# The first scale and shift of a two-layer decoder computed in quarters instead of halves

## The chip, the cores and the metric

One Trainium2 chip, one core. The metric is the device time of one execution in microseconds (us). The engines are TensorE (PE in the rows, its weight loads PEld), VectorE (DVE), ScalarE (ACT), GpSimd (POOL) and SyncE (SP), which here issues most loads.

## The reference

Two decoder layers over 256 prompt tokens and 8 sequences of 4 sample tokens (288 token columns), model width 1024, everything in float32. Layer 0 mixes tokens with retention, layer 1 with a gated delta rule; each is followed by a gated convolutional FFN. Ahead of every sub-layer stands a normalisation whose scale and shift come from a conditioning vector `c`, one per sequence:

```
mod = silu(c) @ w_ada[l] + b_ada[l]
sh1, sc1, g1, sh2, sc2, g2 = split(mod, 6)
h = x * rsqrt(mean(x*x) + EPS) * norm_mix[l]
h = h * (1 + sc1) + sh1
proj = h @ w_ret_in           # q, k, v, gate of the retention
```

The change concerns the first `sh1`, `sc1`, the `h` made of them, and the first columns of `proj`.

## The kernel before

Tokens lie along the free axis: `x` is 8 tiles of 128 channels by 288 tokens. A weight block is 128x1024 float32, 512 KB. For precision each weight block and each activation is split in a high part and a rest (`whi`, `wlo`, `hh`, `hl`), and a product is three rounds of matmuls, `whi`*`hh`, `whi`*`hl`, `wlo`*`hh`, over the 8 channel tiles: 24 matmuls of 128x288. ScalarE makes `whi` (a cast), VectorE `wlo` (a subtraction).

The scale and shift (`ada`) need 14 chunks of 8 blocks. A block gives matmuls into `adaP`, four column groups side by side; when a chunk is complete, ScalarE copies it out (`adaev`), TensorE transposes it (`adaT`), and VectorE adds the bias into `mod`. The retention's first `h` needs two chunks. Chunk 0 holds scale and shift of channel tiles 0 to 3, chunk 1 those of tiles 4 to 7. `modulated` then makes `am` (scale times norm weight), `hs` (the sample tokens, three steps), and for each tile `h` (scaled), `hh` (shifted, cast; ScalarE) and `hl` (the rest; VectorE, GpSimd for the sample tokens). `rb_ret` is the reciprocal root of each token's mean square (`st_ret` its sums).

`first_h` is the start: chunk 0, `h` of tiles 0 to 3, then `EARLY = 3` products begun on these four tiles while chunk 1 is worked off, `h` of tiles 4 to 7, the second half of the begun products. `retention` takes the begun products first: `rt` and `qk` are the rotation of q and k, `qm` masked copies of q, `pA` the scores of head 0, `pv` and `pg` the products of values and gates, `S` blocks of the recurrent state, `pO` its first reader.

The order of the loads is a plan (`plan_weights`); `load` issues them on SyncE in that order as buffers come free: `more` has `RAW_START = 8` places for the start's blocks and then 3, `raw` has 4. `advance` splits weight blocks up to 2 ahead (`LOOK`). Within an engine the order of instructions is settled when the kernel is built: a scheduling layer places what the program records, so an instruction can stand ahead of one recorded earlier. Each engine then runs its list in order.

## Time and profile before

| | us |
|---|---|
| median of 3 runs | 1236.23 (1225.26 to 1239.33) |
| the profiled execution | 1233.65 |
| its span, first to last instruction | 1231.9 |
| TensorE busy | 1164.1, 95% |
| VectorE, ScalarE, GpSimd busy | 870.3, 608.8, 327.7 |
| DMA | 269.08 MB, 218 GB/s over the span |

The profiled execution's own time is 1.75 us more than its span. Times in the rows count from the span's start.

### The profile page before, as it was taken

The page shows a single profiled execution, that of the slowest core. Times are in us where ns is not written, and L with a number is a line of the kernel's source. Part 1 is how long each engine was busy: PE and PEld are TensorE (multiplying, and loading weights), DVE is VectorE, ACT ScalarE, POOL GpSimd, SP SyncE. Part 2 cuts the span into 40 slices and gives each one's busy share as a digit, 9 for nine tenths or more (in the row PEclk, how much of TensorE's full clock was granted, in tenths as well). Part 3 has the DMA queues.
Part 4 walks back from the last instruction along what each step waited for, and adds up shares of the span by engine and source line. Part 5 has one row for each costly group of instructions (what it writes and reads, how often), then busy time and mean ns, then how long its engine had stood idle before and what let it go on. Part 6 is the DMA issues. An engine that isn't in the chain of part 4 may idle for free.

```text
span 1231.9 us, 24934 instructions
## 1 busy us (share of the span) xinstructions
PE 1164.1 (95%) x9486; PEld 1049.1 (85%) x9486; DVE 870.3 (71%) x2003; ACT 608.8 (49%) x1256; POOL 327.7 (27%) x507
## 2 busy tenths in 40 slices
PE   6999999999999999999989998988899899999996
PEld 2879798797969999997777788977889699999996
DVE  3657574765766666667679888797965588777775
ACT  2444534344445544444674645744544365555553
POOL 0213142251302122222252223233222113223232
PEclk9999999999999999999999988988989899999998
DMA  9998696877699556557636641533434897777621
GB/s 365 345 332 324 227 336 233 313 246 242 211 314 393 189 171 190 171 181 259 209 92 211 223 144 63 159 129 115 131 103 129 298 357 239 258 254 253 196 76 56
DMA packets 97480, 269.08 MB, mean 218 GB/s; under 512 B 26816, under 2 KB 29088, under 8 KB 97232
## 3 DMA queue, kind: packets, MB, share of 16 engines
q1 hardware_dynamic: 87456, 234.57, 57.2%
...
q8 instruction: 75, 1.23, 0.4%
q14 instruction: 45, 0.37, 0.1%
...
## 4 chain that ended last, share of the span: by engine, by line
PE 78%; DVE 12%; DMA 3%; ACT 3%; issue 2%; POOL 1%; SPq 0%; POOLq 0%; ACTq 0%; DVEq 0%
PE down L535 17%; PE fg L535 12%; PE fv L535 12%; PE pg L535 4%; PE pv L535 4%; PE adaP L455 4%; PE p L535 3%; PE gv L535 2%; PE gz L535 2%; DVE wlo L417 2%; DVE mp L1332 2%; PE gk L535 2%; PE pO L898 1%; PE pU L917 1%; PE pS L868 1%
## 5 line engine op out<-in xcount | busy, mean ns | idle before, releaser
L417 DVE TENSOR_TENSOR wlo<-more,whi 128x1024 fp32r<-128x1024 f32 x138 | 171.1, 1241 | 74.5 <-ACT whi L416 63.2
L416 ACT CAST whi<-more 128x1024 fp32r<-128x1024 f32 x138 | 144.3, 1047 | 136.5 <-PE down L535 53.1
L417 DVE TENSOR_TENSOR wlo<-raw,whi 128x1024 fp32r<-128x1024 f32 x123 | 155.4, 1267 | 70.6 <-ACT whi L416 48.4
L416 ACT CAST whi<-raw 128x1024 fp32r<-128x1024 f32 x123 | 128.1, 1044 | 133.5 <-PE down L535 32.8
L716 POOL TENSOR_TENSOR x<-x,dt 128x32 f32<-128x32 f32 x159 | 100.6, 634 | 135.2 <-DVE dt L714 134.1
L712 DVE SCALAR_TENSOR_TENSOR x<-down,mod,x 128x256 f32<-128x256 f32 x160 | 76.6, 479 | 51.3 <-PE down L535 50.5
L591 POOL TENSOR_TENSOR fal<-cv,fah 128x288 fp32r<-128x288 f32 x44 | 41.6, 945 | 215.7 <-ACT fah L590 180.7
L535 PE MATMUL down<-fal,whi 128*128 128x288 f32 x352 | 64.0, 294 | 0.0
L535 PE MATMUL down<-fah,whi 128*128 128x288 f32 x352 | 62.3, 294 | 0.0
L535 PE MATMUL down<-fah,wlo 128*128 128x288 f32 x352 | 62.1, 294 | 0.0
L535 PE MATMUL fg<-hh_ffn,whi 128*128 128x288 f32 x352 | 58.9, 300 | 1.2 <-ACT hh_ffn L637 1.2
L918 DVE SCALAR_TENSOR_TENSOR S<-S,pU 128x512 f32<-128x512 f32 x64 | 42.2, 684 | 24.2 <-PE pU L917 24.1
L535 PE MATMUL fv<-hh_ffn,whi 128*128 128x288 f32 x352 | 58.7, 298 | 0.0
L535 PEld LDWEIGHTS fg<-hh_ffn,whi 128*128 128x128 f32 x352 | 50.6, 189 | 5.6 <-ACT hh_ffn L646 2.6
L535 PE MATMUL fg<-hh_ffn,wlo 128*128 128x288 f32 x352 | 55.0, 296 | 0.0
L535 PE MATMUL fv<-hh_ffn,wlo 128*128 128x288 f32 x352 | 54.8, 295 | 0.0
L535 PE MATMUL fv<-hl_ffn,whi 128*128 128x288 f32 x352 | 54.3, 295 | 0.0
L535 PE MATMUL fg<-hl_ffn,whi 128*128 128x288 f32 x352 | 54.0, 295 | 0.0
L535 PEld LDWEIGHTS fv<-hh_ffn,whi 128*128 128x128 f32 x352 | 50.5, 189 | 2.5 <-ACT ftail L947 1.2
L535 PEld LDWEIGHTS down<-fah,whi 128*128 128x128 f32 x352 | 51.8, 188 | 0.8 <-ACT whi L416 0.4
L535 PEld LDWEIGHTS down<-fal,whi 128*128 128x128 f32 x352 | 52.3, 188 | 0.2 <-issue 0.2
L535 PEld LDWEIGHTS down<-fah,wlo 128*128 128x128 f32 x352 | 52.0, 188 | 0.0
...
## 6 DMA issues: line engine op xcount, KB each, us to landing
...
S<-in_sr SPq DMA_DIRECT2D x16, 1024.0 KB, 8.0
out_rs<-S POOLq DMA_DIRECT2D x16, 1024.0 KB, 8.1
...
```

Of the source, the lines that this page charges most:

```text
L416: nc.scalar.copy(hi[:, :c], r)
L417: nc.vector.tensor_tensor(lo[:, :c], r, hi[:, :c].bitcast(F32), ALU.subtract)
L455: nc.tensor.matmul(self.adaP[32 * g : 32 * g + 32, 0:256], lhsT=self.cs[:, k, :], rhs=rv[:, :, g, :], start=(k == 0), stop=(k == KT - 1), ...
L535: self.nc.tensor.matmul(out, lhsT=av[:, k, c0 : c0 + m], rhs=b[:, k, :], start=(k0 == 0 and i == 0), stop=(k1 == kts and i == len(seq) - 1))
L591: (nc.gpsimd if pool_lo else nc.vector).tensor_tensor(lo, src, hi.bitcast(F32), ALU.subtract)
L712: nc.vector.scalar_tensor_tensor(xm[:, :TP], p[:, :TP], g[:, 0:1], xm[:, :TP], ALU.mult, ALU.add)
L716: (nc.vector if gate == 11 and last and m == KT - 1 else nc.gpsimd).tensor_tensor(xv, xv, t, ALU.add)
L868: nc.tensor.matmul(pS, lhsT=kt[:, j, c * P : (c + 1) * P], rhs=vt[:, j, :], start=(j == 0), stop=(j == 1))
L898: nc.tensor.matmul(pO4[32 * g : 32 * g + 32, :], lhsT=qm[:, c, 4 * bb + g, :], rhs=S[bb, c][:, g, :], start=(bb == 0 and c == 0), stop=Fal ...
L917: nc.tensor.matmul(pU, lhsT=kms[g][:, c * P : (c + 1) * P], rhs=vst, start=True, stop=True)
L918: nc.vector.scalar_tensor_tensor(S[bb, c][:, g, :], S[bb, c][:, g, :], gamma4, pU, ALU.mult, ALU.add)
L1332: nc.vector.tensor_tensor(m, Ti[:, 0:k, :].rearrange("p j c -> p c j").unsqueeze(1).to_broadcast([P, w, 8, k]), X[:, 0:k, i:k].rearrange(" ...
```

## The change

The weights of the first scale and shift are laid out anew (`wadq`): four quarters of four blocks, each quarter holding scale and shift of two channel tiles; a block holds two rows of 128 input channels by 512 columns. A quarter's matmuls have 128 columns instead of 256 and are twice as many (`ada_quarter`); per quarter there is one copy, one transpose and two bias additions. `first_h` goes over the quarters: scale and shift, `h` of two tiles, these tiles' part of the products begun so far, then new products from their beginning. `FIRST_W` says how many weights are begun behind each quarter (1, 1, 3, 0), five in all instead of three; they get banks of their own (`START_TAGS`). The start has 15 places for blocks instead of 8. The loads' order is 4 blocks, 1 weight, 4 blocks, 1 weight, 4 blocks, 3 weights, 4 blocks. The split of the first weight of the next phase is kept behind the start's last `hh` and `hl` on its engines (`issue_after`).

```diff
-CST_AT = 4
+CST_AT = 6
-EARLY = 3
-LATE = 1
+FIRST_W = (1, 1, 3, 0)
+EARLY = sum(FIRST_W)
+START_TAGS = ["c", "mm", "s", "mm", "e"]
-RAW_START = 8
+RAW_START = 15
...
-        second, step = ada(1), -(-KT // (EARLY - LATE))
-        plan = [ada(0)]
-        for i in range(EARLY):
-            plan[0] += wl("wri", i, 1) + second[i * step : (i + 1) * step]
+        plan = [[]]
+        for q, n in enumerate(FIRST_W):
+            plan[0] += [("ada", q - 4, k, A["wadq"][4 * q + k]) for k in range(4)]
+            plan[0] += wl("wri", sum(FIRST_W[:q]), n)
...
-            nc.scalar.copy(hi[:, :c], r)
-            nc.vector.tensor_tensor(lo[:, :c], r, hi[:, :c].bitcast(F32), ALU.subtract)
+            with ExitStack() as behind:
+                if self.plan[n][4] and self.plan[n - 1][4] == 0:
+                    for i in self.first_end:
+                        behind.enter_context(self.tc.issue_after(i))
+                nc.scalar.copy(hi[:, :c], r)
+                nc.vector.tensor_tensor(lo[:, :c], r, hi[:, :c].bitcast(F32), ALU.subtract)
...
+    def ada_quarter(self, q, k, r):
+
+        nc = self.nc
+        rv = r.rearrange("p (a g f) -> p a g f", a=2, g=4)
+        for a in range(2):
+            for g in range(4):
+                nc.tensor.matmul(
+                    self.adaP[32 * g : 32 * g + 32, 0:P], lhsT=self.cs[:, 2 * k + a, :], rhs=rv[:, a, g, :],
+                    start=(k == 0 and a == 0), stop=(k == 3 and a == 1), skip_group_check=True,
+                )
+        if k == 3:
+            ev = self.tmp.tile([P, T], F32, tag="t288", name="adaev", bufs=T288)[:, 0:P]
+            nc.scalar.copy(ev, self.adaP[:, 0:P])
+            pt = self.aux("adaT")
+            nc.tensor.transpose(pt[:, 0:P], ev, self.ident)
+            pt = pt[:, 0:P].rearrange("p (m r) -> p m r", r=32)[:, :, 0:9]
+            for m, m0 in ((0, 8 + 2 * q), (2, 2 * q)):
+                bias = self.prm("bada")[:, m0 : m0 + 2].unsqueeze(2).to_broadcast([P, 2, 9])
+                nc.vector.tensor_tensor(self.mod[:, m0 : m0 + 2, :], pt[:, m : m + 2], bias, ALU.add)
...
-        for i in range(EARLY):
-            if i == EARLY - LATE:
-                self.ada_due()
-                self.modulated(0, 0, 1, "ret", *h, rb, KT // 2, KT)
-            w = self.weights("wri")
-            begun.append((self.mmt(f"pe{i}")[:, 0:T], w))
-            self.product(*begun[-1], KT, 0, P, h, 0, KT // 2)
...
+        for q, n in enumerate(FIRST_W):
             self.ada_due()
+            if q == 0:
+                rb = self.now(self.token_rsqrt(self.ssum, 1.0 / DM, "ret"))
+            if q == 2:
+                self.load_cst(rc, "cst_a", nc.scalar, self.mod[:, 2, 0:1])
+            self.modulated(0, 0, 1, "ret", *h, rb, 2 * q, 2 * q + 2)
...
+            for i, (p, w) in enumerate(begun):
+                if q == 3 and i == FREE:
+                    self.hold = False
+                    self.advance()
+                self.product(p, w, KT, 0, P, h, 2 * q, 2 * q + 2)
+            for i in range(n):
+                w = self.weights("wri")
+                begun.append((self.aux(f"pe{len(begun)}", START_TAGS[len(begun)])[:, 0:T], w))
+                self.product(*begun[-1], KT, 0, P, h, 0, 2 * q + 2)
```

What the built order makes of it, at two places. VectorE before, from the second chunk's `mod` on (`wlo<-more` is the third weight's split, the last two those of the fourth and fifth weight):

```order
L468 TENSOR_TENSOR mod<-adaT,prm 128x36 x2
L618 SCALAR_TENSOR_TENSOR am_ret<-mod,prm 128x36
L628 TENSOR_TENSOR hs_ret<-x,am_ret 128x128
L632 TENSOR_TENSOR hs_ret<-hs_ret,rb_ret 128x128
L642 SCALAR_TENSOR_TENSOR h_ret<-x,am_ret,rb_ret 128x256
L417 TENSOR_TENSOR wlo<-more_201,whi 128x1024
L636 TENSOR_TENSOR hs_ret<-hs_ret,mod 128x128
L642 SCALAR_TENSOR_TENSOR h_ret<-x,am_ret,rb_ret 128x256 x3
L648 SCALAR_TENSOR_TENSOR hl_ret<-h_ret,mod,hh_ret 128x256 x4
L417 TENSOR_TENSOR wlo<-more_203,whi 128x1024
L417 TENSOR_TENSOR wlo<-more_205,whi 128x1024
```

VectorE of the changed kernel, quarter 2 from its first `h` to the `mod` of quarter 3 (the three `wlo` are those of the third to fifth weight):

```order
L673 SCALAR_TENSOR_TENSOR h_ret<-x,am_ret,rb_ret 128x256
L667 TENSOR_TENSOR hs_ret<-hs_ret,mod 128x64
L424 TENSOR_TENSOR wlo<-more_144,whi 128x1024
L679 SCALAR_TENSOR_TENSOR hl_ret<-h_ret,mod,hh_ret 128x256
L673 SCALAR_TENSOR_TENSOR h_ret<-x,am_ret,rb_ret 128x256
L424 TENSOR_TENSOR wlo<-raw,whi 128x1024 x2
L679 SCALAR_TENSOR_TENSOR hl_ret<-h_ret,mod,hh_ret 128x256
L499 TENSOR_TENSOR mod<-adaT,prm 128x18 x2
```

Three weight splits instead of one now stand between the two tiles' steps. TensorE before, from the end of chunk 1 (`pe_259`, `pe_295`, `pe_357` are the begun products 1 to 3):

```order
L455 MATMUL adaP<-raw,c 32x256 x4
L455 MATMUL adaP<-more_169,c 32x256 x4
L455 MATMUL adaP<-more_195,c 32x256 x4
L464 MATMUL adaT<-cst,adaev 128x128 x2
L535 MATMUL pe_357<-hh_ret,whi 128x288 x4
L535 MATMUL pe_357<-hl_ret,whi 128x288 x4
L535 MATMUL pe_357<-hh_ret,wlo 128x288 x4
L535 MATMUL pe_259<-hh_ret,whi 128x288
```

TensorE of the changed kernel, around quarter 3 (`pe_251` to `pe_452` are the begun products 1 to 5; the first row waits for the last `hl` of quarter 2):

```order
L566 MATMUL pe_251<-hl_ret,whi 128x288
L566 MATMUL pe_251<-hh_ret,wlo 128x288 x2
...
L566 MATMUL pe_452<-hl_ret,whi 128x288 x6
L566 MATMUL pe_452<-hh_ret,wlo 128x288 x6
L487 MATMUL adaP<-raw,c 32x128 x16
L487 MATMUL adaP<-more_171,c 32x128 x8
L487 MATMUL adaP<-more_173,c 32x128 x8
L495 MATMUL adaT<-cst,adaev 128x128
L566 MATMUL pe_251<-hh_ret,whi 128x288 x2
L566 MATMUL pe_251<-hl_ret,whi 128x288 x2
```

Before, the second chunk's matmuls stand ahead of the third begun product; now those of quarter 3 stand behind all five begun products' work on quarters 0 to 2.

## Rows read from the trace of the kernel before

**Rows 1.** The page: busy us, share of the span and instructions of each engine; and the shares of the chain that ended last, by engine.

```profile
PE 1164.1 (95%) x9486; PEld 1049.1 (85%) x9486; DVE 870.3 (71%) x2003; ACT 608.8 (49%) x1256; POOL 327.7 (27%) x507
...
PE 78%; DVE 12%; DMA 3%; ACT 3%; issue 2%; POOL 1%; SPq 0%; POOLq 0%; ACTq 0%; DVEq 0%
```

**Rows 2.** Windows by stage: stretch and length in us, busy us of each engine with its instructions, granted TensorE clock, busy share of the DMA engines, GB/s.

```profile
7.90:24.30 16.40, 12.27 (x87) 5.11 (x87) 7.29 (x25) 3.58 (x9) 0.21 (x1) 1.00 1.02 393
24.30:39.50 15.20, 13.17 (x95) 7.43 (x95) 7.11 (x18) 4.44 (x9) 1.40 (x5) 0.89 1.02 406
39.50:51.00 11.50, 11.50 (x84) 11.29 (x85) 10.61 (x19) 6.01 (x8) 4.22 (x5) 1.00 0.83 309
51.00:344.00 293.00, 292.43 (x2178) 251.27 (x2176) 186.23 (x326) 129.77 (x226) 83.86 (x104) 1.00 0.77 275
```

**Rows 3.** Timeline of the start: start in us, duration in us, engine, line, operation, output and inputs, shapes, count; in brackets the engine's idle time before it and what ended it.

```profile
7.93 1.08 PE L455 MATMUL adaP<-more,c 128*32 128x256 f32 x8 [7.93 <-ACT sq L606]
9.33 0.20 PEld L455 LDWEIGHTS adaP<-more,c 128*32 128x32 f32 x8 [1.20 <-DMA more<-in_wada]
...
13.20 0.18 PEld L455 LDWEIGHTS adaP<-more,c 128*32 128x32 f32 x2 [1.08 <-DMA more<-in_wada]
...
14.20 1.44 PE L566 MATMUL st_ret<-ones,ssum 128*128 128x1 f32 x6
...
15.68 0.16 DVE L547 TENSOR_SCALAR rsv_ret<-st_ret 128x3 f32<-128x3 f32 x1 [4.54 <-PE st_ret L566]
...
17.47 1.49 PE L575 MATMUL rb_ret<-cst,tr_ret 128*128 128x128 f32 x6
...
18.89 1.25 PE L455 MATMUL adaP<-more,c 128*32 128x256 f32 x16
...
20.48 1.05 ACT L416 CAST whi<-raw 128x1024 fp32r<-128x1024 f32 x1
```

**Rows 4.** Timeline from the last matmuls of chunk 1 to the second half of the begun products; columns as in rows 3.

```profile
33.70 1.24 PE L455 MATMUL adaP<-more,c 128*32 128x256 f32 x15
35.00 0.37 ACT L461 COPY adaev<-adaP 128x256 f32<-128x256 f32 x1 [7.46 <-PE adaP L455]
...
35.42 0.44 PE L464 MATMUL adaT<-cst,adaev 128*128 128x128 f32 x2 [0.48 <-ACT adaev L461]
35.90 0.30 DVE L468 TENSOR_TENSOR mod<-adaT,prm 128x36 f32<-128x36 f32 x2 [7.11 <-PE adaT L464]
...
36.89 0.47 DVE L642 SCALAR_TENSOR_TENSOR h_ret<-x,am_ret,rb_ret 128x256 f32<-128x256 f32 x1
...
37.28 1.22 DVE L417 TENSOR_TENSOR wlo<-more,whi 128x1024 fp32r<-128x1024 f32 x1
38.42 0.28 DVE L636 TENSOR_TENSOR hs_ret<-hs_ret,mod 128x128 f32<-128x128 f32 x1
...
38.94 1.71 ACT L646 ACTIVATE hh_ret<-h_ret,mod 128x256 fp32r<-128x256 f32 x4
...
39.50 1.61 PE L535 MATMUL pe<-hh_ret,whi 128*128 128x288 f32 x10
40.00 1.68 DVE L648 SCALAR_TENSOR_TENSOR hl_ret<-h_ret,mod,hh_ret 128x256 fp32r<-128x256 f32 x4
...
42.12 2.36 DVE L417 TENSOR_TENSOR wlo<-more,whi 128x1024 fp32r<-128x1024 f32 x2 [0.44 <-ACT whi L416]
```

**Rows 5.** Timeline of TensorE: starts of the fourth, fifth and sixth product, and of the scores of head 0.

```profile
44.62 1.21 PE L535 MATMUL p<-hh_ret,whi 128*128 128x288 f32 x8
...
47.81 1.23 PE L535 MATMUL pv<-hh_ret,whi 128*128 128x288 f32 x8
...
51.01 1.23 PE L535 MATMUL pv<-hh_ret,whi 128*128 128x288 f32 x8
...
52.61 1.47 PE L787 MATMUL pA<-qk 128*128 128x256 f32 x8
```

**Rows 6.** Timeline of the rotation of q: two of VectorE's five steps, and GpSimd's part.

```profile
44.83 0.46 DVE L744 TENSOR_TENSOR rt<-pe,cst_a 128x288 f32<-128x288 f32 x1 [0.34 <-PE pe L535]
45.20 0.45 DVE L745 TENSOR_TENSOR rt<-pe,cst_a 128x288 f32<-128x288 f32 x1
...
46.51 0.90 POOL L749 TENSOR_TENSOR qk<-rt,rt 128x288 f32<-128x288 f32 x1 [6.94 <-DVE rt L747]
...
47.49 2.29 POOL L794 TENSOR_TENSOR qm<-qk,cst_b 128x256 f32<-128x256 f32 x2
```

**Rows 7.** TensorE's longest wait behind the first landing (total us, times, longest us, up to 45 us), and two windows behind it, columns as in rows 2.

```profile
PE pe L535 <- ACT hh_ret L637: 2.7, 1, 2.7
...
26.00:29.50 3.50, 3.50 (x19) 1.16 (x18) 1.90 (x3) 1.09 (x2) 0.00 (x0) 0.52 1.03 407
29.50:32.00 2.50, 2.50 (x18) 2.21 (x18) 0.00 (x0) 0.00 (x0) 0.00 (x0) 0.99 1.03 418
```

**Rows 8.** Loads of the recurrent state and of the rotation's table: DMA issues up to 60 us (count, KB each, median us to landing); SyncE's first issue of `S` in its timeline; the reader of `S` in the chain that ended last (start, us).

```profile
S<-in_sr SPq DMA_DIRECT2D x2, 1024.0 KB, 7.9
...
cst_a<-in_cst_a ACTq DMA_DIRECT2D x1, 288.0 KB, 4.7
...
45.53 0.38 SPq L882 DMA_DIRECT2D S<-in_sr  x1
...
71.35 1.72 PE pO L898 x16
```

More of the change, by code (lines that the diff above doesn't have):

```diff
@@ L202, in lay_out @@
     wa = np.concatenate([inp["w_ada"][0], inp["w_ada"][1], inp["w_ada_final"]], 1)
-    wa[:, : 2 * DM] = wa[:, : 2 * DM].reshape(DM, 2, 2, 512)[:, ::-1].transpose(0, 2, 1, 3).reshape(DM, 2 * DM)
-    d["wada"] = wa.reshape(KT, P, 14, 1024).transpose(2, 0, 1, 3).reshape(14 * KT, P, 1024)
+    d["wada"] = wa[:, 2 * DM :].reshape(KT, P, 12, 1024).transpose(2, 0, 1, 3).reshape(12 * KT, P, 1024)
+    w = wa[:, : 2 * DM].reshape(4, 2, P, 2, 4, 256)[:, :, :, ::-1]
+    d["wadq"] = w.transpose(4, 0, 2, 1, 3, 5).reshape(16, P, 1024)
     parts = {
@@ L310, in plan_weights @@
         A = self.A
-        ada = lambda ch: [("ada", ch, k, A["wada"][ch * KT + k]) for k in range(KT)]
+        ada = lambda ch: [("ada", ch, k, A["wada"][(ch - 2) * KT + k]) for k in range(KT)]
         wl = lambda name, i0, n: [("w", name, 0, A[name][i]) for i in range(i0, i0 + n)]
@@ L452, in ada_step @@
             self.adaP = self.aux("adaP", self.ada_tag)
+        if ch < 0:
+            return self.ada_quarter(ch + 4, k, r)
         rv = r.rearrange("p (c g f) -> p c g f", c=2, g=4)
         for g in range(4):
-            nc.tensor.matmul(
+            i = nc.tensor.matmul(
                 self.adaP[32 * g : 32 * g + 32, 0:256], lhsT=self.cs[:, k, :], rhs=rv[:, :, g, :],
@@ L458, in ada_step @@
             )
+            if ch == 2 and k == 0 and g == 0:
+                self.tc.keep_in_program_order(i)
         if k == KT - 1:
@@ L465, in ada_step @@
             pt = pt[:, 0:256].rearrange("p (m r) -> p m r", r=32)[:, :, 0:9]
-            for m, m0, n in ((0, 8 + 4 * ch, 4), (4, 4 * ch, 4)) if ch < 2 else ((0, 8 * ch, 8),):
-                bias = self.prm("bada")[:, m0 : m0 + n].unsqueeze(2).to_broadcast([P, n, 9])
-                nc.vector.tensor_tensor(self.mod[:, m0 : m0 + n, :], pt[:, m : m + n], bias, ALU.add)
+            m0, n = 8 * ch, 8
+            bias = self.prm("bada")[:, m0 : m0 + n].unsqueeze(2).to_broadcast([P, n, 9])
+            nc.vector.tensor_tensor(self.mod[:, m0 : m0 + n, :], pt, bias, ALU.add)
+    def ada_quarter(self, q, k, r):
[16 more added lines that the diff above has]
+                nc.vector.tensor_tensor(self.mod[:, m0 : m0 + 2, :], pt[:, m : m + 2], bias, ALU.add)
     def spawn(self, gen):
@@ L645, in modulated @@
             else:
-                nc.scalar.activation(hi[:, m, :TP], h, AF.Identity, bias=shift[:, i, 0:1])
+                ends = [nc.scalar.activation(hi[:, m, :TP], h, AF.Identity, bias=shift[:, i, 0:1])]
             if lo is not None:
-                nc.vector.scalar_tensor_tensor(lo[:, m, :TP], h, shift[:, i, 0:1], hi[:, m, :TP].bitcast(F32), ALU.add, ALU.subtract)
-        self.ada_due(FILLS[2])
+                ends.append(nc.vector.scalar_tensor_tensor(lo[:, m, :TP], h, shift[:, i, 0:1], hi[:, m, :TP].bitcast(F32), ALU.add, ALU.subtract))
+        if rb_given is None:
+            self.ada_due(FILLS[2])
+        self.first_end = [i.ins for i in ends]
     def h_tiles(self, name):
@@ L662, in first_h @@
         h = self.h_tiles("ret")
[L663 to L667 removed]
         begun = []
         self.hold = True
[L670 to L686 removed]
+        rb = None
+        for q, n in enumerate(FIRST_W):
+            self.ada_due()
+            if q == 0:
[3 more added lines that the diff above has]
+            self.modulated(0, 0, 1, "ret", *h, rb, 2 * q, 2 * q + 2)
+            if q == 3:
+                self.load_cst(rc, "cst_r", nc.scalar, self.mod[:, CST_AT, 0:1])
+                self.load_cst(self.cp, "cst_b", nc.scalar, self.mod[:, CST_AT, 0:1])
+                self.load_cst(self.cp, "prm_b", nc.scalar, self.mod[:, CST_AT, 0:1])
+            for i, (p, w) in enumerate(begun):
[7 more added lines that the diff above has]
+                self.product(*begun[-1], KT, 0, P, h, 0, 2 * q + 2)
         self.hold = False
```

16 lines of the change are left out of this document (1 added, 15 removed).

## The prediction

> **What bounds the kernel now.** I read the page first. TensorE is busy for 95% of the span and carries 78% of the chain that ended last [rows 1], so a stage gains time only where TensorE stands idle or runs slowly. The windows by stage tell where that is [rows 2]: from 51 us to 344 us TensorE is busy for 292.43 of 293.00 us, so whatever the start gains or loses is handed on in full to the first layer's end. From 7.9 to 24.3 us it is busy for 12.27 of 16.40, from 24.3 to 39.5 for 13.17 of 15.20. All its idle time after the first block's landing is thus 4.13 + 2.03 = 6.16 us, 0.5% of the run.
>
> The timeline of the start shows two limits by turns. Blocks land about 1.28 us apart (first use of blocks 2 and 5 at 9.33 and 13.20, three steps) [rows 3], with DMA at 393 to 406 GB/s. Behind the eighth scale-and-shift block, and again behind the sixteenth, one serial chain runs through four engines: copy out, transpose, add the bias, scale, shift, split. Its second run is in [rows 4]: the last matmul of the chunk ends at 33.70 + 1.24 = 34.94, `mod` starts at 35.90 (+0.96), the first `h` at 36.89 (+1.95), and the first product of the second half at 39.50 (+4.56). Of these 4.56 us about 1.14 are one weight split, the `wlo` that stands on VectorE between `h` and `hs` (37.28 to 38.42).
>
> **The yardstick.** I follow both kernels to `pA`, the scores of the first head. Before, it starts at 52.61, behind five full products and half of the sixth (the sixth starts at 51.01) [rows 5]. Eight product matmuls come every 1.06 us (44.62 to 47.81 is 24 of them), 0.133 each. Changed, one more product is done ahead of `pA`: 24 x 0.133 = 3.2, so the old kernel would stand at the same work at 55.8.
>
> **The change, part by part.** It cuts two runs of the serial chain into four shorter ones, and its order decides how far they overlap.
>
> *Chain of a quarter.* The copy has 128 columns instead of 256 (0.37 becomes about 0.25), one transpose replaces two (0.44 becomes about 0.3), and the small steps have 64 columns. I take `mod` at +0.7 and the first `h` at +1.65 from the last matmul of the quarter; +0.96 and +1.95 [rows 4] are the upper bound. Single steps: `h` and `hl` about 0.42 apart (1.68 for four `hl`), `wlo` 1.14 to 1.2, `whi` 1.05, `hh` 0.43.
>
> *Quarter 0.* Its fourth block is used as now, and its matmuls end at about 13.0. ScalarE now has the first weight's `whi` ahead of `adaev`, VectorE its `wlo` ahead of `mod`; this block is the fifth to land (13.20). So `whi` runs 13.2 to 14.25, `mod` waits for `wlo` until 15.5, the row sums `st_ret` (1.44) end at 16.3. The root took 1.79 from its first step (15.68) to `rb_ret` (17.47) [rows 3]; with two small steps put in between, about 2.2: 18.5. `rb_ret` (1.49): 20.0. Then `hs`, two `h`, two `hl`: the last ends at 22.2, and behind it stand two products' matmuls and the rest of quarter 1's last block. Quarter 1 closes at A1 = 23.4.
>
> *Quarter 1.* `mod` +0.7, `hs` to +1.7, then the second weight's `wlo` (1.14), `hs` +2.8, `h` +3.0 and +3.4, `hl` +3.85 and +4.25 to +4.75. Product matmuls wait for that last `hl`; 10 x 0.133 and 19 of the 32 scale-and-shift instructions follow (a block of the same columns costs 0.42, two taking 1.25 with their tail [rows 3]): 1.3 + 1.0. Quarter 2 closes at A2 = A1 + 7.1 = 30.5.
>
> *Quarter 2.* On VectorE three `wlo` now stand inside the quarter, two of them ahead of its last `hl`: `h` +1.65, `hs` +2.05, `wlo` +2.25, `hl` +3.4, `h` +3.8, `wlo` +4.2 and +5.4, `hl` +6.55 to +7.0. ScalarE has two `whi` ahead of the second `hh` and agrees (+5.15). On TensorE 41 matmuls of five products queue behind that `hl`, and the four blocks of quarter 3 behind those: 41 x 0.133 = 5.45, 4 x 0.42 = 1.7, tail 0.25. Quarter 3 closes at A3 = A2 + 7.0 + 7.4 = 44.9. Its blocks landed long before: with five weights ahead of them and 288 KB of `cst_a` [rows 8], the last is the 21st, 7.9 + 20 x 1.28 + 0.7 = 34.2. So the fifteen places keep the queue full, but not what waits for it.
>
> *Quarter 3.* No split stands inside it; the last `hl` runs from +3.4 to +3.85, TensorE has 27 matmuls behind it (3.6): five products done at +7.5, twelve and twenty-four more at +12.3. `pA` needs the rotated q and k, though. VectorE does three `wlo` first: the first `whi` is at +4.4, so to about +8.0 (1.18 each, 2.36 for two [rows 4]). Then five steps of 0.37 for q, and as many for k. GpSimd takes `qk` 0.90 and `qm` 2.29 [rows 6]: q at +9.65 to 10.6, `qm` to 12.9, k to +13.8. So `pA` starts at A3 + 13.85 = 58.75.
>
> *Kept behind.* The sixth weight's split now follows the last `hh` and `hl`. It is done by +5.6 and used from +7.5: no cost while products cover it; without them 2.3 us.
>
> *Clock.* Before 19 us eight passes take 1.08 us, later sixteen take 1.25 [rows 3]: TensorE starts at its lower level. After the longest idle stretch (2.7 us) the granted clock was 0.52 from 26.0 to 29.5, then 0.99 [rows 7]: 3.5 us at 1.2 GHz lose about 1.7. The new order has such a stretch behind the close of quarters 1 and 3 (TensorE waits from about +1.5 to +4, and +1 to +3.4). At the lower level the 2.3 us of quarter 1's tail double, so A2 becomes 32.8 and `pA` 61.05. In quarter 3 the loss of 1.7 fits into TensorE's wait of 1.55 for `qk`. Whether the level falls I can't tell: I take the middle, `pA` at 59.9, 4.1 us late.
>
> *Narrower matmuls.* There are twice as many scale-and-shift matmuls at half the columns. No row shows that width; by columns they cost the same, and if each took as long as a wide one, quarter 3's four blocks would cost 1.7 more and quarter 2's tail 1.0, +2.7 in all, which I keep for the range. The Trainium skill, "TensorE: Matmul & The Clock Gate", section "Back-to-back issue gap", speaks against this split: it says that below some width a matmul's spacing no longer falls with its columns, and puts the floor with decode in microcode at about 62 ns each. By that an estimated block of 16 passes takes 0.99 us, and quarter 3's four blocks 2.3 us more; no run here shows it.
>
> *Later work.* The loads of the recurrent state wait on SyncE behind three weight loads whose places the late `wlo` free, and for the start's memory: `S` was issued at 45.53 and took a median 7.9 us; now about 53, landing 61. Its first reader `pO` is at 71.35 [rows 8], now 75: 14 us to spare, no cost. The products' bank rotation shifts by one; the order of the two FFNs and of the second mixer is the same but for buffer names. Cost 0, and no gain: there is no idle time to win there.
>
> **Sum.** 59.9 - 55.8 = +4.1 us. Against the profiled execution, 1233.65 + 4.1 = 1237.8; that execution is 2.6 under the median of the runs, from which it would be 1240.3. I say 1239. Three runs of one kernel here span 14 us, so about 1% (12 us) is what a measurement can tell from no change.
>
> Bounds of the sum. Below: quarter 2 can't close before its fourth block, the 14th, lands (7.9 + 13 x 1.28 = 24.5, with its matmuls at the lower level 25.3), so `pA` can't start before 25.3 + 14.4 + 13.85 = 53.55, 2.25 us early. Above: the first rival.
>
> **Rivals.**
> (a) *Slower, lower clock all through.* TensorE waits in every quarter and its level stays low until the products run together. Place: quarters 2 and 3. Then the 41 and 27 matmuls, the four blocks and the 36 up to `pA` cost double: A3 = 32.8 + 7.0 + 10.9 + 3.4 + 0.4 = 54.5, `pA` = 54.5 + 3.9 + 7.2 + 9.6 = 75.2, +19.4 us, 1253, or 1.6% slower. It decides from about two thirds of that work at the lower level. For it: idle stretches in four places instead of two. Against: TensorE came back to full level within 3.5 us of steady work at 29.5, and 41 matmuls in a row are 5.45 us of it. The Trainium skill, on the same page ("TensorE: Matmul & The Clock Gate", Part 1), says that the throttled level is the default and activity lifts it; by it both outcomes are open, and the trace agrees as far as it goes (0.52 just after the wait). Chance 0.08.
> (b) *Faster, the landing binds.* If the quarters overlapped freely, A3 would be the landing 34.2 + 0.7, `pA` 48.75: 7.0 us early, 1227 to 1229. For it: the loads are all queued at once, and DMA was the other limit before (share 1.02 [rows 2]). Against: quarter 3's blocks stand behind quarter 2's products on TensorE, whatever landed. Chance 0.09.
> (c) *The change does not do what it says, and no more:* within 1.5 us either way, because the splits take less time between the steps than I think. 1234 to 1237. Chance 0.2.
> (d) *A later stall.* The shifted banks or the later state loads make TensorE wait in the first head, 5 to 12 us: 1244 to 1251. There is no wait on TensorE there now, and 14 us to spare for `S`. Chance 0.08.
> (e) *The forecast,* 1.5 to 9 us later. Chance 0.55.
>
> **Range and chances.** (c), (e) and most of (b) and (d), with some 4 us of scatter of a median, lie in 1229 to 1250. Faster by over 1% needs more than all idle time of the start: 0.04. Slower by over 1%: (a) and the far end of (d), 0.1. The same: 0.86.
>
> **What would show it.** In the changed profile: `mod` of quarter 0 behind `wlo` at about 15.5; three `wlo` between `mod` of quarters 2 and 3; TensorE waiting for `hl` in quarter 2; the last scale-and-shift matmul near 45 although its block landed at 34; `pA` waiting for GpSimd's `qk` at 59 to 61; TensorE without idle from there to the first FFN. I am wrong if quarter 3 closes before 40 us, if a pass of 128 columns takes as long as one of 256, or if idle time appears between 60 and 344 us.

## The result, and the profile after

The changed kernel takes 1246.35 us (median of 4 runs, 1243.47 to 1247.89) against 1233.23 us (4 runs, 1225.26 to 1239.33): 13.1 us more, a ratio of 1.0109 with the 95% interval [1.0079, 1.0139]. That is inside the range of 1229 to 1250, but 7 us above the forecast of 1239, and on the slower side of the bound of 1%, which had a chance of 0.1 (the interval holds both sides of it). The profiled execution has a span of 1245.1 us against 1231.9.

First the page of the changed kernel, for the lines of [rows 1]: busy time of the engines, and shares of the chain that ended last.

```profile
PE 1167.6 (94%) x9614; PEld 1054.8 (85%) x9614; DVE 872.7 (70%) x2015; ACT 608.2 (49%) x1260; POOL 322.9 (26%) x509
...
PE 79%; DVE 10%; DMA 4%; ACT 4%; issue 2%; POOL 1%; ACTq 0%; POOLq 0%; SPq 0%; DVEq 0%
```

TensorE is busy 3.5 us longer than before, though the span is 13.2 us longer. The windows by stage (columns as in [rows 2]; the first three have the bounds of [rows 2], the fourth ends where the first gate product `pg` starts, the fifth where the first layer ends) tell where:

```profile
7.90:24.30 16.40, 13.62 (x141) 9.15 (x141) 7.81 (x26) 3.84 (x10) 0.48 (x1) 1.00 1.03 409
24.30:39.50 15.20, 11.77 (x98) 8.27 (x97) 6.62 (x20) 5.15 (x11) 1.20 (x3) 1.00 0.85 317
39.50:51.00 11.50, 10.73 (x124) 9.71 (x124) 3.18 (x5) 1.64 (x4) 0.00 (x0) 1.00 0.44 161
51.00:73.77 22.77, 19.48 (x138) 17.99 (x137) 15.56 (x30) 10.77 (x19) 7.03 (x14) 0.93 0.87 296
73.77:358.21 284.44, 283.84 (x2074) 240.41 (x2070) 179.14 (x318) 121.97 (x213) 75.84 (x99) 1.00 0.78 269
```

For that fifth stretch, here is the same of the kernel before, from its first `pg` to the end of its first layer:

```profile
64.10:344.02 279.92, 279.33 (x2072) 238.91 (x2070) 179.99 (x318) 122.30 (x212) 79.74 (x99) 1.00 0.77 271
```

Both stretches hold the same matmuls, and TensorE is busy in both but for 0.6 us; yet the changed one takes 284.44 us instead of 279.92, 4.5 us more. `pg` itself is a cleaner yardstick than `pA`, since the same products stand ahead of it in both kernels: 73.77 instead of 64.10, 9.7 us late. (`pA`, with its one product more, starts at 65.50 where I had put the old kernel at 55.8: 9.7 us too.) The rest: first FFN +1.5, second mixer -1.0, last FFN -1.4. Sum +13.3. The last two gains need not belong to the change: in these two stages the changed kernel's trace has 27.3 and 15.8 us at the lower clock, that of the kernel before 44.4 and 21.3.

So there are two losses to explain, 9.7 us up to `pg`, where I had 4.1, and 4.5 us in a stretch without any wait, where I had nothing. For the first, the waits of TensorE from 13 us to `pg` (total us, times, longest), changed kernel, then before:

```profile
PE pe L566 <- ACT hh_ret L677: 2.8, 2, 2.3
PE adaT L495 <- ACT adaev L493: 2.8, 4, 1.4
PE pe L566 <- ACT whi L423: 1.4, 3, 0.6
PE pe L566 <- ACT hh_ret L668: 1.1, 2, 0.7
PE pv L566 <- DVE rt L777: 1.0, 1, 1.0
PE pe L566 <- DVE hl_ret L679: 0.2, 1, 0.2
```

```profile
PE pe L535 <- ACT hh_ret L637: 2.7, 1, 2.7
PE adaT L464 <- ACT adaev L461: 1.0, 2, 0.5
PE pe L535 <- DVE wlo L417: 0.9, 1, 0.9
PE pe L535 <- ACT whi L416: 0.5, 1, 0.5
```

That is 9.3 us of idle time instead of 5.2 (0.2 of it for a landing, not shown), 4.1 more. The one wait `pv <- rt` of 1.0 us was in no step of mine. The other part is the clock. The record of the granted clock of the changed kernel has its first entry, the full level, at 34.7 us, and one dip from 55.2 to 58.6; in the kernel before it is at full level from 19.3, with one dip [rows 7]. (The windows print 1.00 also for stretches ahead of the first entry; there the durations tell.) Rows of TensorE show it, first of the changed kernel, then of e1 below, whose clock rose early (timelines, columns as in [rows 3]):

```profile
12.03 1.08 PE L487 MATMUL adaP<-more,c 128*32 128x128 f32 x16 [0.20 <-DMA more<-in_wadq]
...
33.11 1.17 PE L566 MATMUL pe<-hh_ret,wlo 128*128 128x288 f32 x4
34.20 1.51 PE L487 MATMUL adaP<-more,c 128*32 128x128 f32 x38
36.16 0.33 PE L495 MATMUL adaT<-cst,adaev 128*128 128x128 f32 x1 [0.44 <-ACT adaev L493]
```

```profile
29.76 0.69 PE L566 MATMUL pe<-hh_ret,wlo 128*128 128x288 f32 x4
30.38 1.29 PE L487 MATMUL adaP<-more,c 128*32 128x128 f32 x38
32.10 0.33 PE L495 MATMUL adaT<-cst,adaev 128*128 128x128 f32 x1 [0.43 <-ACT adaev L493]
```

The same four matmuls take 1.17 us in the one and 0.69 in the other. From 13 us to `pg`, 25.1 us lie at the lower level instead of 9.7; without the idle time in them (3.2 us, before 0.2) that is 12.4 us more of work at 1.2 GHz instead of 2.4. Taken as work that would need half the time at the full level, that is a loss of 6.2 us, an estimate. Idle 4.1 + clock 6.2 = 10.3, of which 9.7 are seen. The same two terms, taken off the time from 13 us to `pg` in each of the 14 traces of the table below, leave 39.2 to 42.0 us, so that they account for `pg` to about 1.5 us.

### The profile page after: what moved, and what is told of

Read it like the earlier page. It is cut to its first block, busy times and chain, and to the rows that moved or that the text cites. A ratio compares the mean times of both kernels' runs of the same rounds, so it can differ in the third digit from the quotient of the medians.

```text
span 1245.1 us, 25216 instructions
## 1 busy us (share of the span) xinstructions
PE 1167.6 (94%) x9614; PEld 1054.8 (85%) x9614; DVE 872.7 (70%) x2015; ACT 608.2 (49%) x1260; POOL 322.9 (26%) x509
## 4 chain that ended last, share of the span: by engine, by line
PE 79%; DVE 10%; DMA 4%; ACT 4%; issue 2%; POOL 1%; ACTq 0%; POOLq 0%; SPq 0%; DVEq 0%
PE down L566 18%; PE fg L566 12%; PE fv L566 11%; PE pg L566 4%; PE pv L566 4%; PE adaP L464 3%; PE gv L566 3%; PE p L566 3%; PE gz L566 2%; PE gk L566 2%; DVE mp L1364 2%; PE pU L949 2%; PE pe L566 2%; PE pO L930 1%; DVE wlo L424 1%
## 5 line engine op out<-in xcount | busy, mean ns | idle before, releaser
L424 DVE TENSOR_TENSOR wlo<-raw,whi 128x1024 fp32r<-128x1024 f32 (+1 forms) x122 | 152.5, 1253 | 72.6 <-ACT whi L423 48.3
L423 ACT CAST whi<-raw 128x1024 fp32r<-128x1024 f32 (+1 forms) x122 | 127.0, 1044 | 135.9 <-PE down L566 39.0
L748 POOL TENSOR_TENSOR x<-x,dt 128x32 f32<-128x32 f32 x159 | 95.9, 604 | 133.9 <-DVE dt L746 133.2
L566 PE MATMUL fg<-hh_ffn,whi 128*128 128x288 f32 x352 | 58.5, 299 | 1.2 <-ACT hh_ffn L668 1.2
L566 PE MATMUL fv<-hh_ffn,whi 128*128 128x288 f32 x352 | 58.5, 297 | 1.1 <-ACT whi L423 1.1
L566 PE MATMUL fg<-hh_ffn,wlo 128*128 128x288 f32 x352 | 55.2, 296 | 0.0
L566 PEld LDWEIGHTS fg<-hh_ffn,whi 128*128 128x128 f32 x352 | 50.3, 188 | 5.2 <-ACT hh_ffn L677 2.2
L566 PEld LDWEIGHTS fv<-hh_ffn,whi 128*128 128x128 f32 x352 | 50.3, 189 | 3.2 <-ACT whi L423 1.6
```

The lines of the kernel that those rows point to most:

```text
L423: nc.scalar.copy(hi[:, :c], r)
L424: nc.vector.tensor_tensor(lo[:, :c], r, hi[:, :c].bitcast(F32), ALU.subtract)
L566: self.nc.tensor.matmul(out, lhsT=av[:, k, c0 : c0 + m], rhs=b[:, k, :], start=(k0 == 0 and i == 0), stop=(k1 == kts and i == len(seq) - 1))
L748: (nc.vector if gate == 11 and last and m == KT - 1 else nc.gpsimd).tensor_tensor(xv, xv, t, ALU.add)
```

## The experiments

The table has every run, with what its trace shows: start of `pg`, TensorE's idle time from 13 us to `pg` (waits over 0.15 us), when the granted clock first rises and how long it is at the lower level between 13 us and `pg`, and the stretch from `pg` to the end of the first layer.

| kernel | median us (runs) | ratio to before, 95% | pg | idle | first rise; low | pg to layer's end |
|---|---|---|---|---|---|---|
| before | 1233.23 (4) | | 64.1 | 5.2 | 19.3; 9.7 | 279.9 |
| changed | 1246.35 (4) | 1.0109 [1.0079, 1.0139] | 73.8 | 9.3 | 34.7; 25.1 | 284.4 |
| e1 order restored | 1244.47 (4) | 1.0101 [1.0060, 1.0142] | 70.6 | 11.3 | 19.6; 10.0 | 279.9 |
| e2 + quarter 3 first | 1238.09 (10) | 1.0054 [1.0029, 1.0079] | 67.3 | 9.2 | 20.5; 10.9 | 279.5 |
| e3 halves, five begun | 1236.97 (10) | 1.0046 [1.0027, 1.0065] | 69.8 | 6.7 | 31.9; 22.3 | 280.0 |
| e4 before, new dealing | 1233.83 (10) | 1.0009 [0.9986, 1.0031] | 65.6 | 5.4 | 21.0; 14.8 | 281.2 |
| e5 e2 + rotation free | 1236.60 (10) | 1.0040 [1.0014, 1.0065] | 67.9 | 6.5 | 34.6; 21.6 | 280.1 |
| e6 quarters, three begun | 1235.94 (10) | 1.0019 [0.9998, 1.0041] | 68.3 | 6.1 | 35.8; 22.8 | 280.2 |
| e7 eight places | 1246.07 (2) | 1.0105 [1.0045, 1.0165] | 72.8 | 9.2 | 32.6; 23.1 | 284.0 |
| e8 not kept behind | 1248.18 (2) | 1.0122 [1.0064, 1.0180] | 74.8 | 10.4 | 32.5; 26.3 | 285.4 |
| e9 changed, warmed | 1245.10 (4) | 1.0112 [1.0087, 1.0137] | 69.9 | 10.9 | 7.0; 13.7 | 284.3 |
| e10 before, warmed | 1232.52 (12) | 1.0001 [0.9974, 1.0028] | 65.7 | 5.2 | 4.2; 15.1 | 280.1 |
| e11 e5, warmed | 1234.42 (12) | 1.0028 [1.0011, 1.0044] | 64.8 | 7.9 | 7.1; 11.2 | 279.4 |
| e12 banks restored | 1245.92 (10) | 1.0099 [1.0075, 1.0122] | 73.3 | 10.0 | 32.5; 22.9 | 280.8 |

The kernel before was run beside each set; its medians there were 1231.87 to 1232.20. Ratios are to those runs.

**e1: the order of retention set back.** The start is left as changed.

```diff
-        plan.append(mix(ret[EARLY:], ada(2) + ada(3) + ada(4)) + fill[0])
+        plan.append(mix(ret[3:], ada(2) + ada(3) + ada(4))[EARLY - 3:] + fill[0])
...
         self.begun = [p for p, _ in begun]
+        self.n_mm = 5
```

> The changed kernel with its start as it is, but with retention in the order of the kernel before: the later scale-and-shift blocks are dealt among the weights at the same places as before, and the banks of the products go round as before. From the first gate product (pg) to the row sums of the first FFN (st_ffn) the kernel before takes 279.9 us, the changed one 284.4, both with TensorE busy throughout. Theory A, the loss is the order: the blocks are cut into more pieces between other matmuls, and each cut costs. Then this stretch takes 279.9 +- 0.8 us and the kernel about 1242 us. Rival B, the loss follows from the later start (later loads, clock): the stretch stays at 284.4 +- 0.8 and the kernel at 1246 us.

The stretch is back, in its window:

```profile
70.57:350.44 279.87, 279.28 (x2072) 238.99 (x2070) 179.10 (x318) 123.93 (x216) 79.25 (x99) 1.00 0.76 270
```

Theory A holds for the stretch, and not in e1 alone: the eight traces with the old order of retention (before, e1, e2, e3, e5, e6, e10, e11) have 279.4 to 280.2 us there, whether the clock rose early or late, and the four with the changed one (changed, e7, e8, e9) 284.0 to 285.4. Summed from each matmul's start to the next one's, by operation, the changed kernel's 4.5 us are: `adaP` 15.0 to 16.5, the products 186.2 to 187.2, `pO` from `S` 17.2 to 18.0, `pO` from `at` 9.4 to 10.0, the rest 0.5; in e1 every one of these sums is as before within 0.2. What a cut costs `adaP` can be seen on TensorE's timeline of the changed kernel, where single matmuls of a scale-and-shift block stand between others (two records are the two passes of one matmul):

```profile
152.59 0.62 PE L464 MATMUL adaP<-more,c 128*32 128x256 f32 x2
153.14 0.50 PE L949 MATMUL pU<-vst,km 128*128 128x512 f32 x1
153.57 0.62 PE L464 MATMUL adaP<-more,c 128*32 128x256 f32 x2
154.12 0.49 PE L949 MATMUL pU<-vst,km 128*128 128x512 f32 x1
154.54 0.41 PE L464 MATMUL adaP<-more,c 128*32 128x256 f32 x2
154.56 0.62 PE L930 MATMUL pO<-S,qm 128*32 128x512 f32 x1
154.78 0.39 PE L464 MATMUL adaP<-more,c 128*32 128x256 f32 x2
155.01 0.59 PE L930 MATMUL pO<-S,qm 128*32 128x512 f32 x1
```

and in the kernel before, where two whole blocks stand together:

```profile
134.10 1.07 PE L455 MATMUL adaP<-raw,c 128*32 128x256 f32 x16
134.99 1.90 PE L898 MATMUL pO<-S,qm 128*32 128x512 f32 x16
```

Sixteen passes in a row take 0.89 us to the next start, 0.06 each, because the four column groups run side by side; alone ahead of a `pU`, which has the full width of 128 columns, the two passes of one matmul take 0.55 and 0.55 to theirs. The Trainium skill ("TensorEngine Tiling (Array Packing)", "Key Properties") says that different tiles of the array can run matmuls in parallel; the trace agrees, and shows what a scheduler throws away that puts a matmul of full width between them. Ahead of a `pO`, which works in groups of 32 columns too, a single one takes only 0.02 and 0.23. The stretch has six of the dear kind in the changed kernel and two each in before and e1. With 0.11 for two passes of a run, the four more cost 4 x (0.55 - 0.11) = 1.8 us, near the 1.5 that `adaP` grew by. What lengthens the products and `pO` by the other 3 us was not followed.

The time is only 1.9 us below the changed kernel's, with wide intervals on both; so the 4.5 us are shown in the traced executions, not in the medians. Of every execution the mean granted clock is on record, without the time ahead of its first rise: on average 0.978 in the changed kernel's four, 0.972 in e1's four. In 79 of the 80 executions of the kernel before that ran beside the sets (one at 0.931 left out), each 0.001 less goes with 0.6 us more, so e1's lower clock can hide 3 to 4 us of what it won, an estimate. This run shows something else too: its start is the changed kernel's, instruction for instruction on TensorE up to the sixth product, yet the clock rose at 19.6 instead of 34.7 us, and `pg` came 3.2 us earlier though TensorE waited 2.1 us more.

**e4 and e12: dealing and banks apart.** e4 is the kernel before with the new dealing alone, e12 the changed kernel with the banks' round set back (`self.n_mm = 5`) and the new dealing kept.

```diff
-        plan.append(mix(ret[EARLY:], ada(2) + ada(3) + ada(4)) + fill[0])
+        plan.append(ret[3:5] + mix(ret[5:], ada(2) + ada(3) + ada(4)) + fill[0])
```

> The kernel before in all but one thing: the later scale-and-shift blocks are dealt among retention's weights two weights later, as in the changed kernel. The banks go round as before. Theory A: some of the 4.5 us, 1 to 4 us, come in the stretch from pg to st_ffn (279.9 us before), the start stays as it is, and the time is 1 to 4 us above the kernel before. Rival B: the stretch stays at 279.9 +- 0.8 us. If the stretch stays but e1 wins 4.5 us, the rotation of the banks is the cause.

> The changed kernel with one number set back: behind the five begun products the next product takes the bank that it would take in the kernel before's round, the dealing of the later scale-and-shift blocks stays as changed. From pg to st_ffn the kernel before takes 279.9 us, the changed one 284.4, e1 (dealing and banks set back) 279.9, e4 (dealing alone changed) 281.2. Theory M, the two add up: here 281.2 +- 0.6 us, so that the banks carry 3.2 of the 4.5 us. Rival N, each is enough to spoil the order, or the dealing costs more beside the other banks: 282.5 to 284.4 us. The start is not touched but for the wait of the sixth product, which may be 0.7 us longer as in e1; the time is 1243 to 1245 us under M.

The stretches, first of e4, then of e12:

```profile
65.55:346.72 281.17, 280.58 (x2074) 239.00 (x2070) 178.33 (x318) 122.01 (x210) 78.69 (x99) 1.00 0.77 270
73.29:354.10 280.81, 280.02 (x2075) 238.74 (x2071) 178.55 (x318) 122.96 (x213) 78.79 (x99) 1.00 0.78 269
```

They take 281.17 and 280.81 us, as theory M had it: the dealing costs 0.9 to 1.3 us, and the round of the banks on top of it 3.6 (284.44 less 280.81). The banks without the dealing were not run, so whether they cost 3.6 us by themselves is not shown. e12's time, 1245.92, is above the 1243 to 1245 that went with it; its ten runs lie from 1237.8 to 1249.2, so a median of theirs can't settle 3 us.

**e2: quarter 3 ahead of the three products.** On top of e1:

```diff
-FIRST_W = (1, 1, 3, 0)
+FIRST_W = (1, 1, 0, 3)
```

> As e1, and the three weights of quarter 2 are begun behind quarter 3 instead, so that the four blocks of quarter 3 stand behind 16 product matmuls on TensorE in place of 41. Theory C, the start is late because quarter 3 stands behind the other quarter's products: the last scale-and-shift block ends some 3 to 5 us earlier than in e1 (50.4 us in the changed kernel) and pg starts 2 to 4 us earlier than its 73.8 us; the kernel is 2 to 4 us faster than e1. Rival D, the work ahead of pg binds, whatever its order: pg within 1 us of 73.8, and the kernel as e1.

The transpose of quarter 3 starts at 36.1 us instead of e1's 46.7, `pg` 3.3 us earlier, the time is 6.4 us lower: theory C, with more in the time than its 2 to 4 us and than the trace has (e1's four runs had the lower clock on average, 0.972 against e2's 0.975). Working through 41 product matmuls before quarter 3 closes was the dearest choice of the start's order that these runs price. The transpose of quarter 3 in e2:

```profile
36.06 0.33 PE L495 MATMUL adaT<-cst,adaev 128*128 128x128 f32 x1 [0.44 <-ACT adaev L493]
```

The next wait is in these rows of TensorE and VectorE:

```profile
51.06 1.22 PE L566 MATMUL pe<-hh_ret,wlo 128*128 128x288 f32 x8
54.02 1.17 PE L566 MATMUL pv<-hh_ret,whi 128*128 128x288 f32 x7 [1.74 <-DVE rt L780]
```

```profile
46.40 2.35 DVE L424 TENSOR_TENSOR wlo<-raw,whi 128x1024 fp32r<-128x1024 f32 x2
52.32 0.46 DVE L777 TENSOR_TENSOR rt<-pe,cst_a 128x288 f32<-128x288 f32 x1 [3.57 <-PE pe L566]
```

The sixth product waits 1.74 us for the rotation to read its bank, and the rotation starts only as the last begun product ends (51.06 + 1.22), after 3.57 us in which VectorE had nothing to do.

**e5: the rotation in memory of its own.** On top of e2:

```diff
-            rc = self.pool(ret, "ret_const")
+            rc = self.rc = self.pool(ret, "ret_const")
...
-                qk = rp.tile([P, 2, 2, T], F32, tag="qk", name=f"qk{h}", bufs=1)
+                qk = self.rc.tile([P, 2, 2, T], F32, tag="qk", name=f"qk{h}", bufs=1)
...
-                    t = [rp.tile([P, T], F32, tag=f"rt{i}", name=f"rt{i}", bufs=1) for i in range(4)]
+                    t = [self.rc.tile([P, T], F32, tag=f"rt{i}", name=f"rt{i}", bufs=1) for i in range(4)]
...
-RAW_START = 15
+RAW_START = 12
```

> As e2, but the tiles of the rotation (rt, qk) come from a pool that is open from the beginning, and no longer from memory that the start's places and splits give back; to make room the start has 12 places in place of 15. In e2 the first rt begins only at 52.32 us, when the last begun product ends, though its two inputs are complete some 4 us earlier, and the sixth product waits 1.74 us for it. Theory G, the rotation waits for the memory of the start (all five products read splits that lie there): now rt begins by 50 us, the sixth product has no wait, pg starts 1.5 to 2 us before the 67.25 us of e2, and the time is about 2 us below e2. Rival H, the rotation waits for the products in another way (order on VectorE, the table cst_a): the wait of 1.74 us stays and the time is as e2 within 1 us.

```profile
46.74 0.46 DVE L777 TENSOR_TENSOR rt<-pe,cst_a 128x288 f32<-128x288 f32 x1 [0.77 <-PE pe L566]
```

The rotation starts at 46.74 us, the sixth product follows without a wait at 54.73 (53.68 + 1.05), and the idle time falls by 2.7 us: theory G for the mechanism. `pg` doesn't come earlier, 67.9 for 67.3, because this execution's clock rose at 34.6 instead of 20.5 us (21.6 us at the lower level instead of 10.9); the time is 1.5 us lower, inside both intervals.

**e3 and e6: halves with five, quarters with three.** e3 is the kernel before with `EARLY = 5`, `LATE = 3`, the five banks of `START_TAGS`, 15 places and the old retention order; e6 is the changed kernel with the old retention order and

```diff
-FIRST_W = (1, 1, 3, 0)
+FIRST_W = (1, 1, 0, 1)
```

> The kernel before with its two halves of scale and shift, but with five begun products (two behind the first half, three behind the second half's h), 15 places, and retention's order kept. Theory E, the start is late because of the quarters (four runs of the serial chain, lower clock): here pg stands as in the kernel before, 64.1 us, within 2 us, and the time is within 2 us of the kernel before. Rival F, the five begun products with their loads and splits ahead cost: pg 3 us or more later than 64.1, and the time 3 us or more above the kernel before.

> Quarters of scale and shift, but with three begun products as in the kernel before: one behind quarter 0, one behind quarter 1, one behind quarter 3; 15 places; retention's order as before. Theory I, the quarters themselves cost, since TensorE waits for the copy, the bias and the first split once in each of four runs of the chain instead of two: idle time of TensorE from 13 us to pg is 2 to 4 us above the 5.0 us of the kernel before, and the time 2 to 5 us above it. Rival J, the five begun products are the cost: the idle time is within 1 us of 5.0 us, pg within 1.5 us of 64.1, and the time within 1.5 us of the kernel before.

e3's `pg` is 5.7 us late and its time 4.9 us over, as rival F had it, but only 1.5 us of it are idle time, with one wait of 1.94 us for a later block's landing; 12.6 us more at the lower level are the rest, which neither theory had. e6 has 6.1 us of idle time, 0.9 us more than the kernel before (rival J), yet `pg` is 4.2 us late and the time 3.7 us over (theory I), again with a clock that rose late, at 35.8 us. So five begun products cost by themselves, in the trace mostly by the clock. For the quarters by themselves that is not shown: their ratio's interval, 0.9998 to 1.0041, still holds no change.

**e7 and e8: the other parts undone.** `RAW_START = 8`; and the loop over `self.first_end` taken out.

> The changed kernel with 8 places at the start instead of 15. The forecast held that the places matter little, since quarter 3's blocks wait for TensorE and not for their landing: then pg stands within 1.5 us of what the same clock gives (73.8 us with a late rise of the clock, 70.6 us with an early one as in e1), and the time is within 2 us of the changed kernel's 1246 us. If the landing had carried a gain, pg is later by 3 us or more. A second reading: in the first FFN TensorE waits 1.1 us for a split (whi) in every kernel with five begun products and 15 places and in none with three and 8; if the 15 places cause it, it is gone here, if the five products do, it stays.

> The changed kernel without the edge that keeps the next phase's first split behind the start's last hh and hl. Its three weight splits (whi, wlo) may now stand in front of quarter 3's steps. The forecast put the edge at no cost: then pg and the time stay within 1.5 us of the changed kernel's at the same clock (pg 73.8 us with a late rise, 70.6 us with an early one). If the edge holds the splits back too long, pg comes 1 to 2 us earlier; if it protects quarter 3's chain, pg comes 1 to 3 us later.

Eight places: `pg` 72.8 us with a rise at 32.6, time as the changed kernel; with two runs no effect of the fifteen places can be seen. Without the edge one weight split stands inside quarter 3's steps, and TensorE's wait for `hh` grows from 2.28 us to

```profile
53.55 1.01 PE L565 MATMUL pe<-hh_ret,whi 128*128 128x288 f32 x2 [3.52 <-ACT hh_ret L676]
```

3.52 us, where the changed kernel has

```profile
53.35 0.80 PE L566 MATMUL pe<-hh_ret,whi 128*128 128x288 f32 x2 [2.28 <-ACT hh_ret L677]
```

So the edge protects about 1.2 us, the third of the readings (`pg` 74.8; the time's interval is too wide to add to it). The 1.1 us in the first FFN (TensorE's wait of `fv` for `whi`, 1.09 us at 382.18) stay with eight places, are there in all of e1, e2, e3, e5, e7 to e9, e11 and e12, and are absent in before, e4, e6 and e10: they come with five begun products. Whether by the places on which the later loads then fall, I did not follow.

**e9 to e11: warming TensorE.** Fifteen matmuls whose result nobody reads, in the idle time ahead of the first block, in the changed kernel, the kernel before and e5:

```diff
         nc.vector.memset(self.ones, 1.0)
+        self.warm = self.aux("warm", "s")
+        for _ in range(15):
+            nc.tensor.matmul(self.warm[:, 0:P], lhsT=self.ones, rhs=self.ones, start=True, stop=True)
```

> The changed kernel with 15 matmuls of the tile of ones by itself (128x128, their result is read by nobody) on TensorE in the time before its first block lands, when it has nothing to do. In five of the seven profiles of starts in quarters, TensorE came to its full level only at 32 to 36 us (34.7 us in the changed kernel), in the other two at about 20 us, and I put some 5 us of the late start down to that. Theory K, steady work lifts the level: now it rises before 15 us and pg, 73.8 us in the changed kernel, comes at 67 to 70 us; the time is 4 to 6 us below the changed kernel's 1246 us. Rival L, the late rise belongs to something else (the start of the program, weight loads, chance): the level still rises at 19 to 36 us, pg stays between 70.5 and 74.5 us, and the time within 2 us of the changed kernel's.

> The kernel before with the same 15 matmuls in the idle time ahead of its first block. Theory K: the level rises before 15 us instead of 19 to 21 us, pg comes 1 to 3 us before its 64.1 us, and the time is 1 to 3 us below the kernel before. Rival L: no change, within 1 us. A third reading: the blocks' landing binds up to 13 us and the weights' from there, so that a full clock only makes TensorE wait longer; then the level rises early and pg stays within 1 us of 64.1 us.

> e5 (three weights begun behind quarter 3, retention's order as before, rotation in memory of its own) with the same 15 matmuls ahead of the first block. Theory K: pg comes 3 to 5 us before the 67.9 us of e5 (where the level rose at 34.6 us), and the time is 1231 to 1234 us, level with the kernel before or just under it. Rival L: pg and time as e5, 1236.6 us, within 1.5 us.

```profile
1.04 6.42 PE L1726 MATMUL warm<-ones 128*128 128x128 f32 x30 [1.04 <-DVE ones L1723]
8.05 0.64 PE L487 MATMUL adaP<-more,c 128*32 128x128 f32 x16 [0.58 <-DMA more<-in_wadq]
...
15.40 1.08 PE L487 MATMUL adaP<-more,c 128*32 128x128 f32 x16
```

```profile
7.00:13.80 6.80, 3.37 (x69) 1.94 (x68) 3.12 (x8) 3.26 (x10) 0.00 (x0) 1.00 1.03 413
13.80:24.00 10.20, 8.02 (x66) 6.33 (x66) 5.03 (x20) 1.60 (x4) 0.48 (x1) 0.50 1.03 408
```

In e9 the level rises at 7.0 us (the first block takes 0.64 us instead of 1.08), but TensorE, now twice as fast, is busy for 3.37 of the next 6.80 us, waiting for blocks to land; the level falls at 13.8 us (the same matmuls take 1.08 us at 15.40) and comes back at 24.0. Still, that is 11.4 us less at the lower level and `pg` at 69.9, as theory K had it; the time, 1.3 us lower, is as rival L had it. In e10 the level rises at 4.2 us and is low again from 11.0 to 21.3 and from 24.7 to 31.5, `pg` comes 1.6 us later than in the kernel before, and the time is within 1 us, as rival L had it; that an early rise would be lost again none of the readings had. e11's `pg` is 3.1 us before e5's, as in theory K; its time lies between the two theories', within the intervals of e5's. No version with the change beat the kernel before: the best, e11, is 2.6 us above it, and its interval, 1.0011 to 1.0044, lies above 1.

## Why the prediction was right or wrong

**Right: the direction and the chains.** `mod` of quarter 0 stood behind `wlo` at 15.51 us (15.5), `rb_ret` ran from 18.0 to 19.5 (18.5 to 20.0). Three `wlo` stood between the `mod`s of quarters 2 and 3. From the close of quarter 2 to that of quarter 3 it took 14.6 us (14.4), in the changed kernel and in e1 alike. With e1's early clock the quarters closed at 23.5, 31.7 and 46.3 us, where I had 23.4, 30.5 and 44.9. The idea that quarter 3 stands behind 41 matmuls is what e2 confirmed. Its blocks landed at 37.66 us, not at 34.2, since the places were full; that did not bind.

**Wrong: the term of the clock.** I gave a fall behind quarter 1 either nothing or 2.3 us, and took the middle. In the traced execution TensorE never left the lower level until 34.7 us, so that quarter 1 closed 1.6 us late and quarter 2 5.2 us late: a term of 6.2 us in all up to `pg`. The error was to take the rise at 19.3 us of one execution for a property of the start. In the eight traces of starts in quarters without warming it came at 19.6, 20.5, 32.5, 32.5, 32.6, 34.6, 34.7 and 35.8 us; the two with halves and three products had it at 19.3 and 21.0, e3 with halves and five at 31.9. The Trainium skill ("TensorE: Matmul & The Clock Gate", Part 1) says that the ramp differs from run to run of one kernel; the trace agrees, 19.6 and 34.7 us for one order of instructions. Rival (a), the low clock all through, was right in kind for quarters 0 to 2 and wrong for the 41 and 27 matmuls, which ran at full level but for one dip; the clock cost 6.2 us, not 19.4. Whether quarters or five products make the late rise likelier, or these traces are too few, stays open.

**Wrong: "VectorE does three `wlo` first".** They did stand there, but ended at 58.5 us, and the rotation (of before: [rows 6]) began at 59.67, when the fifth product ended:

```profile
55.03 3.50 DVE L424 TENSOR_TENSOR wlo<-more,whi 128x1024 fp32r<-128x1024 f32 x3 [0.82 <-ACT whi L423]
59.67 0.46 DVE L776 TENSOR_TENSOR rt<-pe,cst_a 128x288 f32<-128x288 f32 x1 [1.14 <-PE pe L566]
60.05 0.45 DVE L777 TENSOR_TENSOR rt<-pe,cst_a 128x288 f32<-128x288 f32 x1
```

```profile
59.21 0.42 PE L566 MATMUL pe<-hh_ret,wlo 128*128 128x288 f32 x2
60.64 1.29 PE L566 MATMUL pv<-hh_ret,whi 128*128 128x288 f32 x8 [1.01 <-DVE rt L777]
```

Its tiles lie in memory that the start's splits give back, and all five products read those (e5 shows it). And the sixth product needed the bank of the first, which the rotation had still to read: 1.01 us of idle time that I had not looked for, since I gave the shifted banks a cost of 0. `pA`, which I had waiting for `qk`, stood behind the seventh product's first half and waited for nothing:

```profile
65.50 1.47 PE L819 MATMUL pA<-qk 128*128 128x256 f32 x8
```

By my own steps it came 6.75 us behind the 58.75 that I had without a fall of the clock: 5.4 us up to the close of quarter 3 (50.3 for 44.9), most of it the clock, and 1.35 from there on (15.2 for 13.85).

**Wrong: the later work at "Cost 0".** I noted that the bank rotation shifts by one, and compared the order of the FFNs and the second mixer, but not that of retention. It cost 4.5 us there (0.9 to 1.3 the dealing, which I had not looked at, 3.6 the banks on top of it), as longer busy time: the sign I had named, idle time between 60 and 344 us, could not have shown it. In the first FFN, whose order is "the same but for buffer names", another 1.1 us came. The loads of `S`, which I had followed at length, made nobody wait: `pO` starts at 80.9 us, with no wait ahead of it. Rival (d), 5 to 12 us with 0.08, came near in size, but its mechanism, a stall, was not the one, nor its place, the first head: of the 4.5 us, 0.3 had come by the second head's first `pg`, 2.5 by the third's and 3.7 by the fourth's.

**The narrow matmuls** cost by columns, as the sum had them:

```profile
48.34 1.08 PE L487 MATMUL adaP<-raw,c 128*32 128x128 f32 x32
49.24 1.06 PE L487 MATMUL adaP<-more,c 128*32 128x128 f32 x32
```

The last 64 passes of quarter 3, two rows, take 1.96 us from 48.34 to their end at 50.30, 0.031 each. By the floor of about 62 ns that the Trainium skill ("TensorE: Matmul & The Clock Gate", "Back-to-back issue gap") gives for decode in microcode they would take 3.97, an estimate with each pass counted as a matmul; the trace does not agree with it.

Worked out anew: idle 4.1, clock 6.2, retention 4.5, first FFN 1.1 are 15.9, less 0.6 by which the first two overshoot the 9.7 us up to `pg`, and 2 that the later stages took less, 13.3 for the 13.2 of the traces. The medians agree in the sum, not in the parts: setting back retention won 1.9 us (e1) and 0.4 (e12, the banks alone) where the traces show 4.5 and 3.6. The change's medians rest on four runs that span 4.4 us; of the untraced executions the mean granted clock is on record, but not when it first rose. Mended one on top of another, retention's order (e1), quarter 3's place (e2), the rotation's memory (e5) and the cold start (e11) take the median from 1246.35 to 1234.42 us and the ratio from 1.0109 to 1.0028.

That the time fell inside the range was in part luck. The forecast's 4.1 us were 2.95 of longer chains and half of 2.3 us of clock; that the idle time grew by 4.1 us as well is chance. The range held two terms that I had put at 1.15 us and at nothing, clock 6.2 and retention 4.5, because it was wide, not because I had seen them.
